# Attention with head pairs in the halves of the array: scores in two banks, values stationary in column halves, gates and y feature-major

## The chip, the core and the metric

The kernel runs on one core of a Trainium2 chip. A core has five engines with their own queues of instructions: PE (TensorE, matrix products; the loads of its stationary operand are listed as PEld), DVE (VectorE), ACT (ScalarE), POOL (GpSimd) and SP (here only a queue of DMAs). Each engine works through its queue in order and waits on semaphores. The metric is the device time of one execution in microseconds; less is better.

## What is computed

The input is 256 tokens of 1024 features. Two layers of a first block, then two of a second, all in float32. The parts that the change touches, from the reference:

```python
# first block, per layer (8 heads of 64 in a and b, 4 of 128 in the memory branch)
qa, ka = partial_rope(a_q), partial_rope(a_k)
ya = moba_attention(qa, ka, va) * silu(a_g)          # causal softmax attention at this length
rel = relu(einsum('bqhd,bsd->bqhs', qi, ki))
idx_score = einsum('bqhs,bqh->bqs', rel, wi)         # its 64 largest keys per query are kept
yb = dsa_attention(qb, kb, vb, qi, ki, wi) * silu(b_g)
ym = memory_attention(m_q, km, vm) * silu(m_g)       # 256 memory rows, no mask
up = einsum('bsnw,nwd->bsnd', stack([ya, yb, ym]), w_branch)
merged = sum(sigmoid(mix) * up)
x = x + merged @ w_out
# second block, per layer: three mixers side by side, then a feed-forward network
o = gt[..., 0:1] * o_cmp + gt[..., 1:2] * o_slc + gt[..., 2:3] * o_win   # NSA mixer, 8 heads of 64
mix = concatenate([o_gla, o_rwkv, o_nsa]) @ w_out
```

## The kernel before, in words

Tokens stand in two tiles of 128 (`tt`). Activations are held feature-major (features on the partitions, 256 tokens in the columns) as operands of the next product, in two parts, high and low, that together carry all bits of the float32 values (class `Feat`, made by `put`, L1395: four transposes on PE, then `split`, one copy on ACT and one subtraction on DVE).

**Weights.** All weights come as one stream in the order in which they are used. `unit` (L250) issues a DMA of 128x1024 on SP's queue into `raw`, ACT makes `whi` (L267) and DVE `wlo` (L244, the helper `tt_`, where most of DVE's elementwise work is recorded). `mm3` (L277) makes three matmuls of each product (L280, L281, L282). A projection is either token-major (`proj_tok`: tokens stationary, 512 weight columns moving) or feature-major (`proj_feat`: weights stationary, the 256 tokens moving).

**Attention of 8 heads of 64** (`causal_attn`, L477). Queries and keys are feature-major, so heads of even number stand on partitions 0 to 63 and those of odd number on 64 to 127. A group is four heads of one parity for the first token tile (128 keys) and two heads for the second (256 keys): two groups for `tt` = 0, four for `tt` = 1. Per group: scores (L490, half of the array's rows), the mask as one more product added into the same bank (L493 causal, L496 index mask), then `softmax_pv` (L456): maximum (L461), its negative (L463), one exponential per head on ACT with the sum of the row beside it (L467), transposes of the unscaled exponentials (L350, the helper `transposed`), a copy to SBUF (L471), and the product with values (L474: transposed exponentials stationary, 64 columns of values moving, result token-major). Branch a and b end in `gate_out` (L500): reciprocal of the sums (L503), y = o / sum, times the gate, and `put`. The memory branch does the same with four heads of 128 (L590). The NSA mixer of block 2 uses `causal_attn` twice per token tile (selected and window), each with its own bank, divisor and sum in SBUF, and a compressed branch (`nsa_compressed`, L1200; products with values L1231).

**The index mask** (`index_mask`, L511): scores (L524) as half-array products, relu on ACT (L527), a weighted sum of eight heads in `iacc` (L532 for the first, L247 for the rest) on DVE, and eight rounds of the eight largest (L544, L545) in `iwork` on DVE.

**PSUM.** Four pools of banks: `pp` 2, `pr` 2, `pa` 3, `pg` 1. `self.ps` takes from `pa`: the result `o` of an attention, the scores of a group and the transposes share its three banks.

**Order.** The program is written as in the source, and a scheduler orders each engine's instructions by priority: a part stands where it is written, moved ahead by `AHEAD[name]` instructions of the section that it is written in (atta -57, attb -195, imask -501, nsa 126, rwkv 38, and so on). So attention, index mask and projections interleave. The table is the same before and after.

Of the kernel before, what the change touches and what calls it, by code (L numbers as in the profile page):

```python
# [113 lines left out]
def consts():  # L114
    c = {}
# [34 lines left out]
class Kern:  # L150
# [48 lines left out]
    def sec(self, name):  # L199
        """a part of the program that is scheduled as if it stood AHEAD[name] instructions earlier"""  # L200
# [5 lines left out]
    def block(self, bufs):  # L206
        """buffers of one block, by tag; streams that run beside each other share no tag"""
# [31 lines left out]
    def accs(self):  # L239
        """[tt][cg] for 1024 columns"""  # L240
# [36 lines left out]
    def mm3(self, out, a, b, start, stop):  # L277
        """out += (ah + al).T @ (bh + bl); the parts carry all bits of the float32 operands"""
# [29 lines left out]
    def proj_feat(self, tag, xT, done, pool, kch=8):  # L308
        """feature-major: out[c] = (x @ W).T for chunks of 128 columns; done(pair, psum[128, 2, 256])"""
# [36 lines left out]
    def transposed(self, ps, srcs):  # L346
        """up to four [128, 128] -> psum [128, n, 128]"""
# [5 lines left out]
    def transp(self, src, dst, tt):  # L353
        """src [128 tok, 512] -> dst[:, 0:4, tt] (float32)"""
# [3 lines left out]
    def bcast(self, ap_row, eng=None):  # L358
        """a row of 1024 for all partitions, in two halves"""
# [6 lines left out]
    def rms(self, xs, g, xT, ps=None, out=None):  # L366
        """x (+= ps) -> split transposes of rmsnorm(x) * g in xT, or the rows in out"""
# [1126 lines left out]
```

## Time and profile before

| | us |
|---|---|
| median of three runs | 1593.73 (1588.67 to 1603.2) |
| span of the profiled execution | 1594.3 |
| PE busy | 1554.3 (97%) |
| PE's stationary loads | 1357.4 (85%) |
| DVE busy | 1018.5 (64%) |
| ACT busy | 719.7 (45%) |

PE's busy share is near the whole; its weight loads run beside its matmuls. A float32 matmul that isn't split by hand is recorded as two. Lengths of matmuls in the trace overlap (their ends are modelled), so what one costs is read from where the next one starts. Next to the engine times the profile has the granted clock of PE, 1 being full speed.

### The profile page before, as it was taken

What the parts mean: (1) busy time and instruction counts of PE and PEld (TensorE: products, weight loads), DVE (VectorE), ACT (ScalarE), POOL (GpSimd) and SP (SyncE); (2) the same over time, 40 slices, a digit from 0 to 9 for tenths busy, and PEclk for the clock granted to TensorE, in tenths of its full rate; (3) what the DMA queues carried; (4) which work ended last, traced back from release to release, by engine and by line L of the source; (5) the groups of instructions that cost most, each with busy time, mean ns of one, the idle gap of its engine ahead of it and who ended that gap; (6) DMA issues with size and microseconds to landing.
All of it is one profiled execution on the core that took longest, in us unless ns stands there. A gap on an engine that the chain in (4) does not pass through costs nothing.

```text
span 1594.3 us, 24848 instructions
## 1 busy us (share of the span) xinstructions
PE 1554.3 (97%) x9868; PEld 1357.4 (85%) x9868; DVE 1018.5 (64%) x1645; ACT 719.7 (45%) x1266; POOL 43.9 (3%) x82
## 2 busy tenths in 40 slices
PE   7999999999999999999999999999999999999998
PEld 6877889989878899979878779999798687789987
DVE  5668556575586565665768685556758786665565
ACT  5544444445544444445644234445346442334451
POOL 0000000000000000010000000000000000100000
PEclk9999999999999999999979999999999998799999
DMA  8642435446534335565212245547353121254661
GB/s 275 229 163 90 153 106 169 162 171 210 182 108 143 107 121 184 191 194 176 91 42 81 71 127 196 188 167 240 129 170 103 54 67 67 67 197 165 200 220 38
DMA packets 72836, 231.78 MB, mean 145 GB/s; under 512 B 8592, under 2 KB 11280, under 8 KB 72720
## 3 DMA queue, kind: packets, MB, share of 16 engines
q1 hardware_dynamic: 67248, 219.74, 41.4%
q10 hardware_dynamic: 5472, 10.46, 2.1%
q8 instruction: 77, 1.26, 0.3%
q14 instruction: 39, 0.32, 0.1%
HBM read 229.12 MB, written 1.05 MB: 144 GB/s over the span
## 4 chain that ended last, share of the span: by engine, by line
PE 86%; DVE 5%; DMA 4%; ACT 3%; issue 1%; POOL 0%; ACTq 0%; SPq 0%; DVEq 0%; POOLq 0%
PE ps L282 21%; PE ps L281 21%; PE ps L280 21%; PE ps L350 5%; PE ps L474 3%; PE ps L490 3%; DMA raw<-in_stream_dram 3%; PE ps L1045 2%; DVE wlo L244 1%; ACT whi L267 1%; PE ps L858 1%; PE ps L880 1%; PE ps L1138 1%; PE ps L826 1%; PE ps L524 1%
## 5 line engine op out<-in xcount | busy, mean ns | idle before, releaser
L244 DVE TENSOR_TENSOR wlo<-raw,whi 128x1024 fp32r<-128x1024 f32 (+2 forms) x396 | 466.7, 1186 | 304.7 <-ACT whi L267 301.9
L267 ACT CAST whi<-raw 128x1024 fp32r<-128x1024 f32 (+2 forms) x396 | 401.5, 1021 | 406.7 <-PE ps L282 164.8
L280 PE MATMUL ps<-xTh,whi 128*128 128x256 f32 (+1 forms) x784 | 224.8, 287 | 4.1 <-ACT whi L267 4.1
L282 PE MATMUL ps<-xTh,wlo 128*128 128x256 f32 (+1 forms) x784 | 224.0, 286 | 0.7 <-DVE wlo L244 0.5
L281 PE MATMUL ps<-xTl,whi 128*128 128x256 f32 (+1 forms) x784 | 223.9, 286 | 0.0
L280 PEld LDWEIGHTS ps<-xTh,whi 128*128 128x128 f32 (+1 forms) x784 | 150.6, 192 | 7.5 <-ACT whi L267 4.5
L282 PEld LDWEIGHTS ps<-xTh,wlo 128*128 128x128 f32 (+1 forms) x784 | 150.4, 192 | 2.8 <-DVE wlo L244 1.2
L281 PEld LDWEIGHTS ps<-xTl,whi 128*128 128x128 f32 (+1 forms) x784 | 150.7, 192 | 0.3
L282 PE MATMUL ps<-whi,hTl 128*128 128x512 f32 (+2 forms) x352 | 135.4, 385 | 0.0
L280 PE MATMUL ps<-whi,hTh 128*128 128x512 f32 (+2 forms) x352 | 135.1, 385 | 0.0
L281 PE MATMUL ps<-wlo,hTh 128*128 128x512 f32 (+2 forms) x352 | 134.6, 382 | 0.0
L282 PE MATMUL ps<-hTh,wlo 128*128 128x256 f32 x448 | 128.9, 288 | 0.0
L280 PE MATMUL ps<-hTh,whi 128*128 128x256 f32 x448 | 128.8, 287 | 0.0
L281 PE MATMUL ps<-hTl,whi 128*128 128x256 f32 x448 | 128.2, 286 | 0.0
L467 ACT ACTIVATE pexp<-ps,nb 128x256 f32<-128x256 f32 (+1 forms) x144 | 59.8, 425 | 66.6 <-DVE nb L463 59.6
L280 PEld LDWEIGHTS ps<-hTh,whi 128*128 128x128 f32 x448 | 85.9, 192 | 0.7
L281 PEld LDWEIGHTS ps<-hTl,whi 128*128 128x128 f32 x448 | 85.8, 191 | 0.7
L282 PEld LDWEIGHTS ps<-hTh,wlo 128*128 128x128 f32 x448 | 85.8, 192 | 0.3
L280 PEld LDWEIGHTS ps<-whi,hTh 128*128 128x128 f32 x352 | 66.1, 188 | 11.9 <-issue 2.0
L281 PEld LDWEIGHTS ps<-wlo,hTh 128*128 128x128 f32 x352 | 66.4, 189 | 11.3 <-issue 0.7
L282 PEld LDWEIGHTS ps<-whi,hTl 128*128 128x128 f32 x352 | 66.3, 188 | 10.9
L280 PE MATMUL ps<-whi,xTh 128*128 128x512 f32 (+1 forms) x176 | 69.8, 397 | 1.4 <-ACT xTh L340 1.3
(447 smaller groups left out, 3076.3 us busy)
## 6 DMA issues: line engine op xcount, KB each, us to landing
raw<-in_stream_dram SPq DMA_DIRECT2D x368, 512.0 KB, 4.0
raw<-in_stream_dram SPq DMA_DIRECT2D x56, 256.0 KB, 3.1
row<-in_ln_w_dram ACTq DMA_DIRECT2D x8, 256.0 KB, 4.7
row<-in_ln_b_dram ACTq DMA_DIRECT2D x8, 256.0 KB, 5.6
raw<-in_stream_dram SPq DMA_DIRECT2D x4, 480.0 KB, 4.6
raw<-in_stream_dram SPq DMA_DIRECT2D x4, 420.0 KB, 3.6
raw<-in_stream_dram SPq DMA_DIRECT2D x4, 396.0 KB, 5.0
P<-in_p_dram ACTq DMA_DIRECT2D x2, 668.5 KB, 5.4
```

What stands on the lines that cost most here:

```text
L244: self.nc.vector.tensor_tensor(out=out, in0=a, in1=b, op=op)
L267: nc.scalar.copy(hi[:, :b - a], raw)
L280: mm(out, a[0], b[0], start=start, stop=False)
L281: mm(out, a[0], b[1], start=False, stop=False)
L282: mm(out, a[1], b[0], start=False, stop=stop)
L350: self.nc.tensor.transpose(pt[:, j], s, self.ident)
L467: nc.scalar.activation(p3[:, i], sv[:, i], AF.Exp, bias=nb[:, i:i + 1], scale=scale, accum_out=den[:, h:h + 1])
L474: nc.tensor.matmul(o[:, ocol(h)], ps[:, i * nk + k, :], vt(k, h), start=first and i == 0 and k == 0, stop=last and i == nh - 1 and k == nk ...
L490: nc.tensor.matmul(s3[:, i], qT[pr, h // 2], kT(pr, h, 128 * nk), start=i == 0, stop=False)
L524: nc.tensor.matmul(s3[:, i], iqT[pr, h // 2, 128 * tt:128 * tt + 128], ikT[pr, :n], start=i == 0, stop=i == hs - 1)
L826: mm(ps[:, c], st[pr, c, 128 * tt:128 * tt + 128], ar4[tt][pr, :, c, :], start=c == 0, stop=c == 1)
L1045: mm(ps[:, tt, c], E[pr, c, sl], E[pr, c, sl], start=tt + c == 0, stop=tt + c == 2)
```

## The change

- `causal_attn` takes heads in pairs: scores of both parities go into two banks, in turn. `softmax_pv` becomes `probs`: the reciprocal of the row sums (L476), in block 2 times the mixer's gate, is multiplied into the exponentials (L480, one instruction a head) before their transposes. The product with values (L510) has 64 columns of values stationary in one half of the array's columns and 128 tokens moving; even heads give partitions 0 to 63 of the result and odd ones 64 to 127. The result is feature-major.
- `gate_proj`: the three gates of a block-1 layer are projected feature-major. `gate_out` multiplies the feature-major result by them and splits it, with no transposes of y.
- `nsa_direct`: selected and window attention add into one bank; ACT copies the sum. `nsa_compressed` scales its probabilities, makes its products in column halves (32 of them), adds and splits; no `put` of yn, and no section "ofn".
- `index_mask` issues the scores of both parities in turn, into two banks.
- Comments and docstrings are taken out.

Between the orders of before and after: 48 transposes of yb and 16 of yn are gone; 288 weight matmuls of 512 columns became 576 of 256; 384 matmul records of values have 128 moving columns instead of 64; on DVE there are 144 more scalings and 56 reciprocals in place of 20. The DMAs are the same.

```diff
-    def softmax_pv(self, sv, heads, nk, scale, vt, o, ocol, den, first, last):
+    def probs(self, sv, coef, scale):
 ...
-        for i, h in enumerate(heads):
-            nc.scalar.activation(p3[:, i], sv[:, i], AF.Exp, bias=nb[:, i:i + 1], scale=scale,
-                                 accum_out=den[:, h:h + 1])
-        pt = self.transposed(self.ps, [p[:, 128 * j:128 * j + 128] for j in range(nh * nk)])
+        for i in range(nh):
+            nc.scalar.activation(p3[:, i], sv[:, i], AF.Exp, bias=nb[:, i:i + 1], scale=scale, accum_out=den[:, i:i + 1])
+        rd = self.sm.tile([128, 4], F32, name="rd")
+        nc.vector.reciprocal(rd[:, :nh], den[:, :nh])
+        if coef is not None:
+            self.tt_(rd[:, :nh], rd[:, :nh], coef, ALU.mult)
+        for i in range(nh):
+            nc.vector.tensor_scalar(p3[:, i], p3[:, i], rd[:, i:i + 1], None, op0=ALU.mult)
+        pt = self.transposed(self.ps, [p[:, 128 * j:128 * j + 128] for j in range(nh * n // 128)])
         ps = self.u("ptsb", 4, 128)
         nc.vector.tensor_copy(ps, pt)
-                nc.tensor.matmul(o[:, ocol(h)], ps[:, i * nk + k, :], vt(k, h),
-                                 start=first and i == 0 and k == 0, stop=last and i == nh - 1 and k == nk - 1)
 ...
+            sv = [self.ps(hs, 128 * nk) for _ in par]
+            for i in range(hs):
+                for a, pr in enumerate(par):
+                    h = g + 2 * i + a
+                    nc.tensor.matmul(sv[a][:, i], qT[pr, h // 2], kT(pr, h, 128 * nk), start=i == 0, stop=False)
 ...
+            pT = [self.probs(sv[a], coef[:, g + a:g + 2 * hs:2] if coef is not None else None, 0.125) for a in range(2)]
+            for i in range(hs):
+                for k in range(nk):
+                    for a, pr in enumerate(par):
+                        nc.tensor.matmul(o[pr, g // 2 + i], v(k, g + 2 * i + a), pT[a][:, i * nk + k],
 ...
-        self.tt_(y.rearrange("p (h d) -> p h d", h=nh), o.rearrange("p (h d) -> p h d", h=nh),
-                 rd[:, :nh, None].to_broadcast([128, nh, d]), ALU.mult)
-        self.tt_(y, y, g2, ALU.mult)
-        ysT.put(y, 0, tt, 0.5)
+        for p in range(2):
+            self.tt_(y[:, 2 * p:2 * p + 2], o[:, 2 * p:2 * p + 2], g2[p][:, :, sl], ALU.mult)
+        self.split(y, ysT.h[0][:, :, sl], ysT.l[0][:, :, sl], 0.5)
 ...
-            g2 = self.tok_proj(f"{n}g{l}", hT, "g", self.silu2)
+            g2 = self.gate_proj(f"{n}g{l}", hT)
 ...
+            self.nc.scalar.copy(out[tt], o)
 ...
-            for g in range(2):
-                mm(oc[:, g], pT[:, g], vc[g], start=g == 0, stop=g == 1)
+            for j in range(4):
+                for g in range(2):
+                    mm(oc[64 * g:64 * g + 64, j], vc[g][:, j], pT[:, g], start=j == 0, stop=j == 3)
```

How the order changes, at three places of the first layer (a row is a line, an operation, output<-inputs, shape, and how many follow each other; a float32 matmul is one row here and two records in the trace).

PE, where branch a begins, before: index scores (L524) stand among the weight matmuls (L280 to L282) and the first scores (L490).

```order
L524 MATMUL ps<-ikT,iqT 128x256
L280 MATMUL ps<-whi,hTh 128x512
L524 MATMUL ps<-ikT,iqT 128x256
L281 MATMUL ps<-wlo,hTh 128x512
L282 MATMUL ps<-whi,hTl 128x512
L524 MATMUL ps<-ikT,iqT 128x256 x4
L280 MATMUL ps<-whi,hTh 128x512
L281 MATMUL ps<-wlo,hTh 128x512
L524 MATMUL ps<-ikT,iqT 128x256
L490 MATMUL ps<-kT,qT 128x128 x4
```

The same place after: index scores (now L533) and the scores (now L499) with their causal mask (L502).

```order
L533 MATMUL ps<-ikT,iqT 128x128 x8
L533 MATMUL ps<-ikT,iqT 128x256 x6
L499 MATMUL ps<-kT,qT 128x128 x4
L502 LDWEIGHTS negb
L502 MATMUL ps<-causb,negb 128x512
L533 MATMUL ps<-ikT,iqT 128x256 x2
L280 MATMUL ps<-whi,hTh 128x512
L281 MATMUL ps<-wlo,hTh 128x512
L499 MATMUL ps<-kT,qT 128x128 x4
```

The index scores moved together, 14 of a layer's 16 in one block, behind the end of the gates' projection; the first two groups' scores follow each with its mask.

PE, a little later, after: the products with values of the first pair (L510, `ptsb` being the transposed probabilities) and the scores of the second pair (L499); what each waits for is in brackets.

```order
L350 MATMUL ps<-c_ident,pexp 128x128 [waits DVE_49,Activation_49]
L510 MATMUL ps<-ptsb,v 64x128 [waits PE_49]
L350 MATMUL ps<-c_ident,pexp 128x128 [waits DVE_49] x3
L499 MATMUL ps<-kT,qT 128x256 [waits Activation_49]
L499 MATMUL ps<-kT,qT 128x256
L502 LDWEIGHTS negb
L502 MATMUL ps<-causb,negb 128x2x128
L281 MATMUL ps<-wlo,hTh 128x512
L510 MATMUL ps<-ptsb,v 64x128 [waits DVE_49]
L510 MATMUL ps<-ptsb,v 64x128 x6
L499 MATMUL ps<-kT,qT 128x256 [waits PE_49]
L499 MATMUL ps<-kT,qT 128x256
```

One product stands by itself and seven follow later, where before each group had its four together. The second bank's scores stand behind the first bank's and behind the products.

DVE in that stretch, before: between the rounds of the first index selection (L544, L545) stand pieces of the weights (wlo).

```order
L544 MAX m_663<-iacc 128x8
L545 MATCH_REPLACE iwork<-m_663,iacc 128x128
L244 TENSOR_TENSOR wlo<-raw,whi 128x1024
L544 MAX m_663<-iwork 128x8
L545 MATCH_REPLACE iwork<-m_663,iwork 128x128
L544 MAX m_663<-iwork 128x8
L545 MATCH_REPLACE iwork<-m_663,iwork 128x128
L544 MAX m_663<-iwork 128x8
L545 MATCH_REPLACE iwork<-m_663,iwork 128x128
L244 TENSOR_TENSOR wlo<-raw,whi 128x1024
```

After: the rounds of both selections (now L555, L556) stand among the softmax's pieces.

```order
L480 TENSOR_SCALAR pexp<-pexp,rd 128x128 x4
L469 TENSOR_SCALAR nb<-mx 128x4
L555 MAX m_663<-iwork 128x8
L247 SCALAR_TENSOR_TENSOR iacc<-irel,wi,iacc 128x256
L483 COPY ptsb<-ps 128x512
L556 MATCH_REPLACE iwork<-m_663,iwork 128x128
L555 MAX m_715<-iacc 128x8
L555 MAX m_663<-iwork 128x8
L556 MATCH_REPLACE iwork<-m_715,iacc 128x256
L476 RECIPROCAL rd<-den 128x4
L556 MATCH_REPLACE iwork<-m_663,iwork 128x128
L480 TENSOR_SCALAR pexp<-pexp,rd 128x128 x4
```

No wlo stands from the first index sum to the end of the second selection; before, one stood every few rows.

## Rows read from the trace of the kernel before

**Rows 1.** The page's part 1: busy time, share of span, instructions of each engine.
```profile
PE 1554.3 (97%) x9868; PEld 1357.4 (85%) x9868; DVE 1018.5 (64%) x1645; ACT 719.7 (45%) x1266; POOL 43.9 (3%) x82
```

**Rows 2.** The page's part 4: the chain that ended last, by engine.
```profile
PE 86%; DVE 5%; DMA 4%; ACT 3%; issue 1%; POOL 0%; ACTq 0%; SPq 0%; DVEq 0%; POOLq 0%
```

**Rows 3.** Stretches: length, busy PE, PEld, DVE, ACT, POOL, granted clock, DMA share, GB/s.
```profile
110.00:160.00 50.00, 50.00 (x269) 38.07 (x268) 40.92 (x112) 23.99 (x56) 0.58 (x2) 1.00 0.30 102
809.30:833.20 23.90, 23.23 (x97) 19.57 (x96) 13.92 (x27) 9.39 (x20) 0.00 (x0) 0.50 0.07 23
1345.20:1375.90 30.70, 30.59 (x107) 24.03 (x107) 13.00 (x25) 2.75 (x6) 1.64 (x1) 0.50 0.05 21
```

**Rows 4.** Timeline of PE at 159 us: start, length, line, shape, count.
```profile
159.19 0.40 PE L282 MATMUL ps<-whi,hTl 128*128 128x512 f32 x1
159.42 0.60 PE L350 MATMUL ps<-c_ident,yb 128*128 128x128 f32 x4
159.78 0.48 PE L280 MATMUL ps<-whi,hTh 128*128 128x512 f32 x1
```

**Rows 5.** Timeline of PE at 180 us: narrow weight matmuls and single scores.
```profile
179.88 0.28 PE L282 MATMUL ps<-hTh,wlo 128*128 128x256 f32 x1
180.00 0.28 PE L280 MATMUL ps<-hTh,whi 128*128 128x256 f32 x1
...
180.63 0.39 PE L281 MATMUL ps<-hTl,whi 128*128 128x256 f32 x1
...
181.36 0.38 PE L282 MATMUL ps<-hTh,wlo 128*128 128x256 f32 x1
```

**Rows 6.** Timeline of PE from 102 us: index scores of a block-1 layer.
```profile
102.12 0.49 PE L524 MATMUL ps<-ikT,iqT 64*128 64x128 f32 x2
...
102.97 0.49 PE L524 MATMUL ps<-ikT,iqT 64*128 64x128 f32 x2
...
117.79 1.14 PE L524 MATMUL ps<-ikT,iqT 64*128 64x256 f32 x8
```

**Rows 7.** Timeline of PE at 188 us: one group's products, another's scores.
```profile
187.80 1.10 PE L474 MATMUL ps<-v,ptsb 128*128 128x64 f32 x8
188.83 1.16 PE L490 MATMUL ps<-kT,qT 64*128 64x128 f32 x8
```

**Rows 8.** Timeline of PE at 906 us: alternating column halves, and what follows.
```profile
905.58 0.66 PE L949 MATMUL ps<-r_M,r_WU 128*64 128x128 f32 x8
906.17 1.10 PE L955 MATMUL ps<-r_WU,r_M 128*128 128x64 f32 x8
```

**Rows 9.** Timeline of DVE at 130 us: weights, reciprocal, copy of transposes.
```profile
129.98 1.21 DVE L244 TENSOR_TENSOR wlo<-raw,whi 128x1024 fp32r<-128x1024 f32 x1
...
131.50 0.19 DVE L503 RECIPROCAL rd<-den 128x8 f32<-128x8 f32 x1
131.63 0.69 DVE L471 COPY ptsb<-ps 128x512 f32<-128x512 f32 x1
```

**Rows 10.** Timeline of ACT at 130 us: exponentials of one softmax.
```profile
129.71 0.37 ACT L467 ACTIVATE pexp<-ps,nb 128x128 f32<-128x128 f32 x1
...
130.06 0.36 ACT L467 ACTIVATE pexp<-ps,nb 128x128 f32<-128x128 f32 x1
```

**Rows 11.** Line L532: durations in ns (minimum, median, maximum), forms.
```profile
L532 DVE TENSOR_SCALAR iacc<-irel,wi x4: 286/312/335, 105.8 to 455.0; 128x128 f32<-128x128 f32 x2, 128x256 f32<-128x256 f32 x2
```

**Rows 12.** Line L467: who waited for it (us, times).
```profile
  PEld ps L350: 8.2, 25
```

**Rows 13.** Busy DVE (last row third) from 100 us on iacc, iwork, mx, ptsb.
```profile
100.00:160.00 60.00, 8.59 (x24) 0.58 (x2) 1.00 0.32 109
...
100.00:160.00 60.00, 12.31 (x48) 1.00 0.32 109
...
100.00:160.00 60.00, 5.11 (x12) 1.00 0.32 109
...
100.00:160.00 60.00, 6.43 (x48) 5.89 (x48) 4.12 (x6) 1.00 0.32 109
```

More of the change, by code (lines that the diff above doesn't have):

```diff
@@ L448, in tok_proj, with gate_proj @@
         return dst
+    def gate_proj(self, tag, hT):
+        g2 = [self.u("g", 2, 256) for _ in range(2)]
+        self.proj_feat(tag, hT, lambda p, ps: self.silu2(g2[p], ps), self.next_pool())
+        return g2
     def silu2(self, dst, ps):
-        t = self.u("tg")
+        t = self.u("tg", 2, 256)
         self.nc.scalar.activation(t, ps, AF.Tanh, scale=0.5)
         self.stt(dst, t, 1.0, ps, ALU.add, ALU.mult)
-    def softmax_pv(self, sv, heads, nk, scale, vt, o, ocol, den, first, last):
+    def probs(self, sv, coef, scale):
         nc = self.nc
-        nh = len(heads)
+        nh, n = sv.shape[1], sv.shape[2]
         mx = self.sm.tile([128, 4], F32, name="mx")
@@ L465, in softmax_pv, with causal_attn @@
         p3 = p.rearrange("p (h k) -> p h k", h=nh)
-        for i, h in enumerate(heads):
-            nc.scalar.activation(p3[:, i], sv[:, i], AF.Exp, bias=nb[:, i:i + 1], scale=scale,
-                                 accum_out=den[:, h:h + 1])
-        pt = self.transposed(self.ps, [p[:, 128 * j:128 * j + 128] for j in range(nh * nk)])
+        den = self.sm.tile([128, 4], F32, name="den")
+        for i in range(nh):
[7 more added lines that the diff above has]
+        pt = self.transposed(self.ps, [p[:, 128 * j:128 * j + 128] for j in range(nh * n // 128)])
         ps = self.u("ptsb", 4, 128)
         nc.vector.tensor_copy(ps, pt)
-        for i, h in enumerate(heads):
-            for k in range(nk):
-                nc.tensor.matmul(o[:, ocol(h)], ps[:, i * nk + k, :], vt(k, h),
-                                 start=first and i == 0 and k == 0, stop=last and i == nh - 1 and k == nk - 1)
-    def causal_attn(self, qT, kT, v, tt, o, den, mask=None):
+        return ps
+    def causal_attn(self, qT, kT, v, tt, o, first, last, mask=None, coef=None):
         nc = self.nc
@@ L481, in causal_attn @@
         hs = 4 // nk
[L482 removed]
+        par = (slice(0, 64), slice(64, 128))
         for g in range(0, 8, 2 * hs):
[L484 to L498 removed]
@@ new lines, in causal_attn @@
+            for i in range(hs):
+                for a, pr in enumerate(par):
+                    h = g + 2 * i + a
+                    nc.tensor.matmul(sv[a][:, i], qT[pr, h // 2], kT(pr, h, 128 * nk), start=i == 0, stop=False)
+            for s3 in sv:
+                if mask is None:
+                    nc.tensor.matmul(s3[:, :, 128 * tt:128 * tt + 128], self.negb,
+                                     self.causb[:, None, :].to_broadcast([128, hs, 128]), start=False, stop=True)
+                else:
+                    nc.tensor.matmul(s3, self.negb, mask[:, None, :].to_broadcast([128, hs, 128 * nk]), start=False, stop=True)
@@ L1204, in nsa_compressed @@
         for tt in range(2):
-            acc = out[tt]
             den = self.sm.tile([128, 8], F32, name="n_cden")
@@ L1221, in nsa_compressed @@
             self.tt_(cf, cf, gate[:, 0], ALU.mult)
+            self.tt_(s, s, cf[:, :, None].to_broadcast([128, 8, 15]), ALU.mult)
             pc = self.u("n_pc", 2, 4, 32)
@@ L1228, in nsa_compressed @@
             nc.scalar.copy(pT, pt)
-            oc = self.ps(2, 4, 64)
-            for g in range(2):
-                mm(oc[:, g], pT[:, g], vc[g], start=g == 0, stop=g == 1)
-            t = self.u("n_t", 4, 2, 64)
-            c3 = cf.rearrange("p (j g) -> p g j", g=2)
-            for g in range(2):
-                self.tt_(t[:, :, g], oc[:, g], c3[:, g, :, None].to_broadcast([128, 4, 64]), ALU.mult)
-            self.tt_(acc, acc, t.rearrange("p j g d -> p (j g d)"), ALU.add)
+            oc = self.ps(4, 128)
+            for j in range(4):
+                for g in range(2):
+                    mm(oc[64 * g:64 * g + 64, j], vc[g][:, j], pT[:, g], start=j == 0, stop=j == 3)
+            self.tt_(out[tt], out[tt], oc, ALU.add)
+            sl = slice(128 * tt, 128 * tt + 128)
+            self.split(out[tt], yT.h[0][:, :, sl], yT.l[0][:, :, sl])
     def block2_layer(self, l, xT):
@@ L1251, in block2_layer @@
         yr, yg = self.c3("yr"), self.c3("yg")
-        yn = [self.u("yn") for tt in range(2)]
+        yn = [self.u("yn", 4, 128) for tt in range(2)]
         qT, kT, KX, vt, gc = self.nsa_inputs(l, xT)
@@ L1265, in block2_layer @@
         with self.sec("cpd"):
-            self.nsa_compressed(qT, gc, kc, vc, yn)
-        with self.sec("ofn"):
             yT = Feat(self, 4, "xT")
-            for tt in range(2):
-                yT.put(yn[tt], 0, tt)
+            self.nsa_compressed(qT, gc, kc, vc, yn, yT)
         with self.sec("h1"):
```

76 lines of the change are left out of this document (25 added, 51 removed).

## The prediction

> **What bounds the kernel now.** I read the engine totals first [rows 1]: PE is busy 1554.3 of 1594.3 us, DVE 64% and ACT 45% of the span. The chain that ended last [rows 2] says the same: 86% of it is PE, 5% DVE. So the time is PE's list of instructions, plus 40 us in which PE waits. Then I looked at the one stretch of a block-1 layer where DVE is nearly as full: from 110 to 160 us [rows 3] PE is busy all 50 us, and DVE 40.92. There the index mask, the attention of branch a and the splitting of the weights (wlo) share DVE. In block 2 two stretches of 24 and 31 us run at a granted clock of 0.50 [rows 3], the lower level of 1.2 GHz, while PE is busy nearly all the time; what lengthens them is paid double. The profiled span of 1594.3 us stands 0.6 us above the median of the runs, so differences worked out on the trace go against the median, 1593.7, as they are.
>
> **Part 1: what PE no longer does.** The transposes of y go: 48 of yb and 16 of yn. A group of four between weight matmuls takes PE from 159.42 to 159.78, 0.09 us each [rows 4]; sixteen such groups are about 6 us, and 7 with what they cost on entry. I take -7.
>
> The gates change shape: 288 weight matmuls of 512 columns become 576 of 256. Pitches are 0.23 us [rows 4] and 0.12 us [rows 5], so 576 x 0.119 - 288 x 0.231 is +2.
>
> The products with values: a group of 8 records (four matmuls of 64 columns, two records each because they are plain float32) takes 0.91 to 1.1 us; the one at 187.80 holds PE until 188.83 [rows 7]. There are 48 such groups, some 46 us. After the change a pair of groups is 16 records of 128 columns into alternating column halves, issued as one single (2 records) and one run of 14, as the excerpt of the order on the first pair's products shows. The nearest row is the stretch of L949, which has just this form: 8 records from 905.58 to 906.17 [rows 8], that is four pitches of 0.11 and 0.15 for entering and leaving. Seven pitches and 0.15 are 0.93 us; the single has to be entered and left by itself, about 0.46. 24 x (0.46 + 0.93) = 33, so -12. If only one half runs at a time, 16 x 0.11 + 0.3 a pair gives 50, so +4; if the single costs nothing extra, -15.
>
> Here a rule of the Trainium skill speaks against the change. The row shows 0.15 us around the L949 group. The page TensorEngine Tiling (Array Packing), section Key Properties, says that changing the tiling mode drains TensorE, and the groups that did not change mode before now do so twice a pair. It gives no price; with another 0.28 for each of the 48 entries, what the lone half-row group at 188.83 pays beyond its columns (1.16 - 8 x 0.11, [rows 7]), the part's gain would be about 0 instead of -12.
>
> The scores: the code alternates the two row halves, but o, two score banks and the transposes share the three banks of one PSUM pool. In the same excerpt the scores into the second bank stand behind those into the first, their mask and the products, with a wait of their own. So a group still costs what it costs now, 1.1 us (1.16 with its modelled end) at 188.83 [rows 7], except where both banks happen to be free. The index scores are such a place. Before, most were singles between weight matmuls: a single and a weight matmul take 0.85 us [rows 6], so the single costs 0.62, and a layer's sixteen about 8.5. After, 14 of them stand in one block and alternate halves: by the run at 117.79, 8 records of 256 columns in 1.14 [rows 6], the block is about 2.6. That is -6 a layer. Against it, in branch b the first pair's scores become eight singles among weight matmuls instead of four and a group: from 180.63 to 181.36 less 0.12 makes 0.61 each [rows 5], four times 0.61 less 1.1, and the same once more in part for block 2: about +2.5 a layer. Sum -7, bounds -3 and -12.
>
> The compressed branch's 8 wide matmuls become 32 small ones: +1. In all PE has 23 us less to do (-7 + 2 - 12 - 7 + 1), bounds -6 and -34.
>
> **Part 2: what DVE gets.** Every probability is now scaled before its transpose: a reciprocal, and 64 multiplications of 128 columns and 80 of 256. The same form, an elementwise multiply with a scalar per row, took 0.286 and 0.335 us in L532 [rows 11]. Against this the divisions at the end of a branch and the n_t sums go, and the gate products read half as much. Net about +20 us on DVE, at a share of 64%. Over most of the kernel PE's queue of weight matmuls hides that. Two places don't.
>
> First, branch a of each block-1 layer. In the order before, wlo pieces stand between the pieces of the index mask. After, there is none between the one ahead of the index block and the one behind the second imask. DVE has there the index sums and the selection, 8.59 + 12.31 us less about 1.6 counted in both [rows 13], the maxima of six softmax calls 5.11, five of the six copies of 4.12 [rows 13], and newly some 5 us of scaling, 1 of reciprocals, 0.8 and 0.7 for y and its split, 1 of rope: about 36 us by durations. An instruction's successor starts some 0.08 us before its end (131.50 with 0.19, next at 131.63 [rows 9]), times 90 that is 7: 29 us, and with the wlo that ends it 30 to 31 after the first index score. PE has in the same stretch 48 weight matmuls (11.1), the index block (2.6 and some 1.5 of waits for the relu), six groups of scores with masks (7), transposes (2.6) and values (2.8): about 26 to 27 before it needs that wlo. PE waits 4.5 us, twice: +9, bounds 0 (if the weights' buffers carry it over) and +16 (if the selection's steps wait for each other).
>
> Second, the softmax chain. Before, the first transpose could follow the first exponential; the pitch of these is 0.35 us [rows 10]. Now it follows all of a group's exponentials, a reciprocal of 0.19 [rows 9] and a scaling: about 1.5 us later with four heads of 128, 1.1 with two of 256, in 56 calls. The order gives part of it back, since in branch b 27 to 31 narrow weight matmuls stand where 20 stood. The trace of before shows 8.2 us of waits for pexp in 25 places [rows 12]; I take half as much again, +4, bounds 0 and +20.
>
> In block 2 the pairs come later: two or three are still to come when the last weight matmuls are gone, before it was two. They share DVE with rwkv there. I take +2, bounds -5 and +15, the half of the longer slow-clock stretch.
>
> The edit's other pieces (ACT splits y from SBUF instead of PSUM, four copies of yn) lie on ACT at 45% [rows 1] and cost nothing as long as no transpose waits for them; uncovered they would be 16 x 0.69 by the copy of that size at 131.63 [rows 9], 11 us. DMA is the same list.
>
> **Sum.** -23 + 9 + 4 + 2 = -8, so about 1585 us.
>
> **Rivals.** (1) The cover holds: the wlo pieces made ahead and the reordered weight matmuls hide both DVE places. For it: DVE has a third of its time free and the order moved fillers to where the transposes are. Against it: no wlo in 29 us of DVE work. Then -23 and 0 to +3 remain: 1571 to 1574. (2) Slower: the longer softmax chain is exposed everywhere. In each of 56 calls a reciprocal and scalings now stand behind a wlo of 1.2 us [rows 9] where one comes between exponentials and transposes. Uncovered by half, 0.65 us a call, it is +36 instead of +4: 1594 - 23 + 9 + 36 + 2 = 1618. It decides when a call's exposure passes 0.5 us (28 + 11 - 23 = +16, one per cent). For it: the two halves of a pair share three banks, so a pair's chain can't be started ahead; against it: only 8.2 us are waited there now. (3) The change doesn't do what it says: each of the 48 entries into column halves costs another 0.28 us and eats the gain, so -11 of PE work against +15: about 1598. Against it stands the L949 row [rows 8], where 8 records took 0.59 us against 1.03 in the whole array [rows 7].
>
> **How the numbers follow.** Forecast 0.42, between 1575 and 1597 by its own terms; rival 1 0.25; rival 2 0.16; rival 3 0.17. About one per cent, 16 us, is what a measurement of this kernel tells from no change. Faster by more than that (under 1578) are nearly all of rival 1 and a fifth of the forecast: 0.32. Slower (over 1610) is rival 2: 0.15. The rest, 0.53, is within it. The range of 1565 to 1613 leaves out the best end of rival 1 and most of rival 2, about 2 in 10.
>
> **What would show it.** Right: no L350 on yb or yn; the values' runs of 14 records in about 0.9 us; index scores in a block of about 3 us soon after 100 us; DVE over 90% busy there and PE waiting 4 to 5 us for a wlo just behind it, twice; waits of transposes for pexp of 10 to 15 us in all. Wrong: values at 1.5 us or more a pair (rival 3), waits for pexp of 30 us and more (rival 2), or none for that wlo (rival 1); and a granted clock of 0.50 in block 2 over another length than 24 and 31 us would move the time by half the difference.

## The result, and the profile of the changed kernel

The changed kernel takes 1613.45 us in the median of 11 runs (1604.5 to 1616.6), the kernel before 1596.9 beside it on the same chip. The ratio is 1.0093, with an interval of 1.0068 to 1.0118: 15 us slower, where 9 us faster was forecast. Medians, ratios and parts of time are here and below those of fast runs alone; a run over 1.5% above the fastest of its kernel counts as slow. The profiled execution has a span of 1614.7 us against 1594.3.

The engine totals (the page's part 1) and the chain that ended last (part 4; here it is followed back through 63% of the span only, so its shares are small):

```profile
PE 1560.7 (97%) x10140; PEld 1361.4 (84%) x10140; DVE 1034.8 (64%) x1825; ACT 722.5 (45%) x1270; POOL 46.0 (3%) x82
```

```profile
PE 53%; DVE 4%; DMA 3%; ACT 2%; issue 1%; POOL 0%; ACTq 0%; DVEq 0%; POOLq 0%; SPq 0%
```

Against [rows 1] DVE has 16 us more (20 were forecast) and keeps its share. PE's busy time should have fallen by 23 and rose by 6. Busy time hides how fast the work ran; the stretches tell it. Columns as in [rows 3]: length, busy PE, PEld, DVE, ACT, POOL, granted clock, DMA share, GB/s. The last lines are those of the stretches that lie at the lower level in the changed kernel:

```profile
110.00:160.00 50.00, 47.49 (x253) 36.17 (x252) 40.48 (x122) 22.80 (x47) 0.29 (x1) 1.00 0.31 106
170.00:180.70 10.70, 10.70 (x75) 9.36 (x73) 5.59 (x6) 4.24 (x5) 0.00 (x0) 1.00 0.51 177
180.70:187.50 6.80, 6.80 (x23) 5.15 (x23) 1.56 (x4) 0.97 (x6) 0.00 (x0) 0.50 0.20 66
795.00:802.00 7.00, 7.00 (x31) 5.26 (x30) 3.97 (x6) 3.89 (x8) 0.00 (x0) 0.51 0.26 84
812.00:826.00 14.00, 13.62 (x50) 9.00 (x49) 8.76 (x22) 2.95 (x9) 2.23 (x4) 0.51 0.00 0
918.00:935.00 17.00, 13.83 (x48) 11.62 (x49) 9.06 (x18) 2.09 (x6) 3.32 (x2) 0.50 0.04 15
1266.00:1287.00 21.00, 21.00 (x82) 15.04 (x80) 10.57 (x30) 6.23 (x18) 2.66 (x4) 0.51 0.00 1
1314.00:1324.00 10.00, 10.00 (x44) 9.30 (x42) 5.00 (x16) 3.19 (x12) 0.40 (x1) 0.50 0.00 1
1365.00:1396.00 31.00, 28.59 (x104) 22.61 (x104) 13.17 (x25) 2.64 (x6) 2.08 (x2) 0.50 0.00 1
```

With a second one like that at 180.70, at 519, and some short ones, 125 us lie at 0.50; before it was 77. Block 1 had none before: in the kernel before, the stretches 180.70 to 187.50 and 519 to 526 have 1.00 (46 and 51 matmuls on PE, here 23 and 29 in about as long).

What that costs can be read from the runs alone, since each lists its span and mean granted clock. Call (1 - clock) x span the time lost. Over 179 runs of the ten kernels with ten or more of them, a run's span stands above its own kernel's mean by 0.78 us for each us that its lost time stands above that kernel's mean (correlation 0.97). So I divide a kernel's difference to before (medians: span 1593.2, lost 33.5, 82 runs) into 0.8 times the difference in lost time, "the clock", and "the rest", what remains at equal clock. That the factor holds from kernel to kernel as it does from run to run is assumed. For the changed kernel: span 1611.7, lost 58.0, so +18.5 us, of which 0.8 x 24.5 = 20 are the clock, and the rest is -1. The forecast had +2 for the clock and -10 for everything else. Both parts are off, the first by 18 us, the second by 9.

### The profile page after: what moved, and what is told of

Read it like the earlier page. It is cut to its first block, busy times and chain, and to the rows that moved or that the text cites. A ratio compares the mean times of both kernels' runs of the same rounds, so it can differ in the third digit from the quotient of the medians.

```text
span 1614.7 us, 25573 instructions
## 1 busy us (share of the span) xinstructions
PE 1560.7 (97%) x10140; PEld 1361.4 (84%) x10140; DVE 1034.8 (64%) x1825; ACT 722.5 (45%) x1270; POOL 46.0 (3%) x82
## 4 chain that ended last, share of the span: by engine, by line
PE 53%; DVE 4%; DMA 3%; ACT 2%; issue 1%; POOL 0%; ACTq 0%; DVEq 0%; POOLq 0%; SPq 0%
PE ps L280 12%; PE ps L282 12%; PE ps L281 12%; PE ps L350 3%; DMA raw<-in_stream_dram 3%; PE ps L1057 2%; PE ps L499 2%; DVE wlo L244 1%; PE ps L510 1%; PE ps L892 1%; PE ps L870 1%; ACT whi L267 1%; PE ps L838 1%; PE ps L1150 1%; PE ps L881 1%
## 5 line engine op out<-in xcount | busy, mean ns | idle before, releaser
L244 DVE TENSOR_TENSOR wlo<-raw,whi 128x1024 fp32r<-128x1024 f32 (+2 forms) x396 | 467.5, 1190 | 319.1 <-ACT whi L267 317.8
L280 PE MATMUL ps<-xTh,whi 128*128 128x256 f32 (+1 forms) x784 | 224.3, 286 | 4.8 <-ACT whi L267 4.6
L282 PE MATMUL ps<-xTh,wlo 128*128 128x256 f32 (+1 forms) x784 | 223.7, 286 | 0.8 <-DVE wlo L244 0.8
L281 PE MATMUL ps<-hTl,whi 128*128 128x256 f32 x640 | 184.9, 289 | 0.0
L282 PE MATMUL ps<-hTh,wlo 128*128 128x256 f32 x640 | 184.8, 289 | 0.0
L280 PE MATMUL ps<-hTh,whi 128*128 128x256 f32 x640 | 184.5, 288 | 0.0
L280 PEld LDWEIGHTS ps<-xTh,whi 128*128 128x128 f32 (+1 forms) x784 | 150.4, 192 | 9.2 <-ACT whi L267 5.0
L282 PEld LDWEIGHTS ps<-xTh,wlo 128*128 128x128 f32 (+1 forms) x784 | 150.4, 192 | 3.2 <-DVE wlo L244 1.5
L282 PEld LDWEIGHTS ps<-hTh,wlo 128*128 128x128 f32 x640 | 124.0, 194 | 1.8 <-issue 0.8
L281 PEld LDWEIGHTS ps<-hTl,whi 128*128 128x128 f32 x640 | 124.1, 194 | 1.4 <-issue 0.4
L280 PEld LDWEIGHTS ps<-hTh,whi 128*128 128x128 f32 x640 | 124.1, 194 | 1.2 <-issue 0.6
L281 PE MATMUL ps<-wlo,hTh 128*128 128x512 f32 (+2 forms) x256 | 95.1, 372 | 2.1 <-DVE wlo L244 2.1
L282 PE MATMUL ps<-whi,hTl 128*128 128x512 f32 (+2 forms) x256 | 95.6, 373 | 0.0
L280 PE MATMUL ps<-whi,hTh 128*128 128x512 f32 (+2 forms) x256 | 94.6, 372 | 0.0
L280 PE MATMUL ps<-whi,xTh 128*128 128x512 f32 (+1 forms) x176 | 69.7, 397 | 3.8 <-ACT xTh L340 2.6
L281 PE MATMUL ps<-wlo,xTh 128*128 128x512 f32 (+1 forms) x176 | 69.1, 392 | 0.9 <-DVE wlo L244 0.9
L282 PE MATMUL ps<-whi,xTl 128*128 128x512 f32 (+1 forms) x176 | 69.3, 394 | 0.1
L467 DVE TENSOR_REDUCE mx<-ps 128x2 f32<-128x512 f32 (+1 forms) x56 | 38.2, 688 | 38.7 <-PE ps L502 19.9
```

What stands on the lines that cost most here:

```text
L244: self.nc.vector.tensor_tensor(out=out, in0=a, in1=b, op=op)
L280: mm(out, a[0], b[0], start=start, stop=False)
L281: mm(out, a[0], b[1], start=False, stop=False)
L282: mm(out, a[1], b[0], start=False, stop=stop)
L467: nc.vector.tensor_reduce(out=mx[:, :nh], in_=sv, axis=AX.X, op=ALU.max)
```

## The experiments

The suspects in the order in which they came: the place of the added scores in branch b, the place of NSA in block 2, the two score banks, the scaling of the probabilities. The table gives for each kernel the ratio to before with its interval, and the two parts, in us, as above. (From run to run of one kernel the rest scatters by 1 to 2 us; a factor of 0.7 or 0.9 in place of 0.8 would shift it by up to 2.5 us. On the four chips of the experiments the kernel before has the same at equal clock within 0.4 us.)

| kernel | median us | ratio | interval | clock | rest |
|---|---|---|---|---|---|
| the changed kernel | 1613.5 | 1.0093 | 1.0068-1.0118 | +20 | -1 |
| e1_attb: branch b later | 1598.9 | 1.0033 | 1.0003-1.0064 | +15 | -11 |
| e2_nsa: NSA earlier | 1606.4 | 1.0106 | 1.0030-1.0182 | +14 | -2 |
| e3_before_pair: before, two banks | 1599.4 | 1.0056 | 1.0012-1.0101 | -3 | +7 |
| e4_noscale: no scaling | 1595.8 | 1.0014 | 0.9969-1.0058 | +6 | -6 |
| e5_block1: block 1 only | 1599.7 | 1.0058 | 1.0020-1.0096 | +9 | -4 |
| e6_block2: block 2 only | 1608.3 | 1.0071 | 1.0037-1.0105 | +13 | 0 |
| e7_block1_attb: e5 and e1 | 1583.2 | 0.9931 | 0.9891-0.9971 | +3 | -15 |
| e8_block2_noscale: e6, no scaling | 1601.2 | 1.0049 | 1.0010-1.0089 | +1 | +5 |
| e9_block2_act: e6, scaling on ACT | 1619.0 | 1.0142 | 1.0092-1.0193 | +20 | +4 |
| e10_nsa170: e1, NSA earlier | 1593.1 | 0.9972 | 0.9945-0.9999 | +12 | -14 |
| e11_nsa200: e1, NSA earlier still | 1586.7 | 0.9980 | 0.9939-1.0021 | +4 | -12 |
| e12_before_table: before, e11's table | 1598.1 | 1.0007 | 0.9967-1.0047 | 0 | +3 |

A trace, on the other hand, is of one execution, and executions of one kernel differ in clock (the kernel before from 0.967 to 0.990). So a stretch's clock in one trace against that in another says little by itself; the table decides.

**Branch b's scores.** One entry of the table that sets the order is changed.

```diff
-AHEAD = dict(... attb=-195, ...)
+AHEAD = dict(... attb=-135, ...)
```

> The changed kernel with one number of the order table altered (attb from -195 to -135): in branch b of both block-1 layers the first pair's eight scores stand together instead of alternating one by one with narrow weight matmuls; block 2 is ordered as in the changed kernel. Theory C (stretches in which PE is poorly filled make the granted clock fall, and the falls are the loss): the two stretches of 6.8 us at 0.50 near 181 and 519 us are gone, 3.4 us each, and with them seven singles at some 0.5 us a layer; about 14 us faster than the changed kernel, 1600 us. Theory D (the longer softmax chain and DVE are the loss): within 3 us of the changed kernel, 1611 to 1616 us.

In the changed kernel the first pair's eight scores of branch b stand one by one among narrow weight matmuls. The timeline of PE (start, length, line, operation, shape, records):

```profile
177.09 0.48 PE L499 MATMUL ps<-kT,qT 64*128 64x128 f32 x2
177.50 0.39 PE L281 MATMUL ps<-hTl,whi 128*128 128x256 f32 x1
177.82 0.48 PE L499 MATMUL ps<-kT,qT 64*128 64x128 f32 x2
...
180.01 0.48 PE L499 MATMUL ps<-kT,qT 64*128 64x128 f32 x2
180.42 0.39 PE L282 MATMUL ps<-hTh,wlo 128*128 128x256 f32 x1
180.74 0.79 PE L499 MATMUL ps<-kT,qT 64*128 64x128 f32 x2
181.46 0.58 PE L280 MATMUL ps<-hTh,whi 128*128 128x256 f32 x1
181.97 0.79 PE L499 MATMUL ps<-kT,qT 64*128 64x128 f32 x2
```

Each single and its weight matmul take 0.73 us, and from the sixth on 1.23: there the granted clock falls to 0.50, and stays there for 6.8 us. The same happens in the second layer at 519. The trace shows no wait of PE in the 10.7 us before the fall (ends of matmuls are modelled). With the entry changed, the eight stand together, and the same part of both layers keeps its clock (stretches of e1_attb):

```profile
170.00:190.00 20.00, 19.40 (x157) 16.99 (x156) 15.15 (x34) 10.78 (x31) 0.00 (x0) 1.00 0.35 118
505.00:530.00 25.00, 24.33 (x185) 20.71 (x185) 17.01 (x42) 12.85 (x37) 0.00 (x0) 1.00 0.33 107
```

So the entry is worth 15 us of span, 4 by the clock and 10 at equal clock in the table. The two traces show where: the last matmul on the y of block 1 (`ps<-ysh,wlo`) starts at 667.3 us in the changed kernel and at 653.3 in e1_attb, so 14.0 of the 15 us arise before block 2, half in each layer. Of the 7 us of a layer 3.4 are half speed; eight singles at 0.61 [rows 5] in place of one row of 16 records that takes 1.09 us (171.32 to 172.41 in e1_attb) are 3.8, an estimate.

**NSA earlier in block 2.**

```diff
-AHEAD = dict(... nsa=126, ...)
+AHEAD = dict(... nsa=190, ...)
```

> The changed kernel with the NSA attention of block 2 moved ahead (nsa from 126 to 190), so that all its pairs lie among weight matmuls and none among rwkv's last steps. Theory C: the time at 0.50 in block 2 (85 us without the ends, 68 before the change) shrinks to 60 or less, 10 to 17 us faster than the changed kernel, about 1600 us. Theory D: the chain of a pair is as long, its waits now fall among weight matmuls; at most 5 us faster, 1608 us or more.

Only four runs stand behind it, so the interval is wide. The medians say that a third of the clock's cost goes (20 to 14) and the rest stays; whether the kernel is faster than the changed one these runs don't tell. Theory C's 10 to 17 us did not come, and the trace, that of the slowest of the four, has no less time at 0.50 in block 2 (a clock of 0.91 from 770 to 1400 us, 0.92 in the changed kernel).

**Two score banks alone, in the kernel before.**

```diff
-        for gi, heads in enumerate(groups):
-            s3 = self.ps(hs, 128 * nk)
 ...
+            sv = [self.ps(hs, 128 * nk) for _ in par]
+            for i in range(hs):
+                for a, pr in enumerate(par):
+                    h = g + 2 * i + a
+                    nc.tensor.matmul(sv[a][:, i], qT[pr, h // 2], kT(pr, h, 128 * nk), start=i == 0, stop=False)
 ...
```

> The kernel before with one part of the change alone: scores of both parities issued in turn into two banks, everything behind them as before (no scaling, transposes of y, token-major gates). Its order has 64 single half-array scores among other matmuls, before 32. Theory C: the clock falls in branch b and in block 2 as after the change; 10 to 15 us slower than before, 1607 to 1612 us. Theory D: the softmax chain is the old one, so no more than the singles themselves, 32 at 0.2 to 0.5 us less what alternating halves save: 1594 to 1604 us.

It has 64 single half-array scores (those of the index mask among them) where before has 32, and it is 7 us slower at equal clock, but its clock is no lower than before's in the median. 32 singles at 0.61 in place of eight groups at 1.1 would be some 11 us, an estimate from [rows 5] and [rows 7]; so the singles are enough to explain the loss, and two banks by themselves gain nothing. It has the same eight singles in branch b as the changed kernel, and its trace (that of its lowest clock, 0.961) falls at the same place of the first layer, for 3.4 us:

```profile
182.56 0.69 PE L488 MATMUL ps<-kT,qT 64*128 64x128 f32 x2
183.18 0.58 PE L282 MATMUL ps<-hTh,wlo 128*128 128x256 f32 x1
```

```profile
182.80:186.20 3.40, 3.40 (x14) 2.69 (x14) 1.56 (x4) 1.07 (x2) 0.00 (x0) 0.51 0.00 0
```

In its second layer, with the same eight from 514 to 520 us, it does not fall. Counted over all fourteen traces: where six to eight of these scores stand one by one (the changed kernel, e2, e3, e4, e5), the clock falls at them in nine of ten layers; where four do or none (the nine others), in none of eighteen. In block 2 the singles of e3_before_pair (22, before has 2) leave the median clock as it was, so singles alone are no rule.

**Without the scaling.** This kernel leaves out the division by the sums of the softmax.

```diff
-for i in range(nh):
-    nc.vector.tensor_scalar(p3[:, i], p3[:, i], rd[:, i:i + 1], None, op0=ALU.mult)
```

> The changed kernel without the 144 scalings of the probabilities (the division by the row sums is left out, so the output is not the reference's); the transposes again follow the exponentials. Theory D: the loss goes, 15 us or more faster than the changed kernel, under 1599 us. Theory C: the waits that the scalings cause go, some 3 us a block-1 layer and as much in block 2, but the order still has 42 single scores; 4 to 10 us faster, 1603 to 1609 us.

It gains 17.7 us on the changed kernel by the medians of the span, 13 of them the clock. That is the time that theory D had. But the order changes with it too (42 singles), so it doesn't tell whether the work on DVE, the longer chain or the order did it.

**One block at a time.** The other block keeps the code of before (its softmax, gates and, in e6, the transposes of yb; in e5 those of yn).

> The change in block 1 alone (branches a, b, memory, index scores, gates); block 2's mixers as before, ordered as in the kernel before. Theory C (the loss is the granted clock, most of it in block 2): block 1 has at equal clock 2 to 3 us less a layer and pays 3.4 us a layer for the stretch at 0.50 in branch b, so 1592 to 1600 us, the same as before. Theory S (the loss is the single half-array scores and the waits of block 1): 8 us or more slower than before, 1603 us or more.

> The change in block 2 alone (NSA mixer); block 1 as before, ordered as in the kernel before. Theory C: most of the loss, 10 to 18 us slower than before, 1605 to 1613 us, with more time at 0.50 than the 65 us of before between 790 and 1400 us. Theory S: within 5 us of before, 1590 to 1600 us.

Block 1 is worth +5 us, block 2 +13, and the sum of 18 is that of the whole change. Block 1's share is a clock cost of 9 with a rest of -4, and its profile has the two stretches at 180 and 518. Block 2's share is all clock. In its trace, that of its lowest clock (0.964), the two attention stretches stand at 0.86 and 0.79, where the kernel before has 0.90 (790 to 940) and 0.88 (1240 to 1385). Stretches of e6_block2, of the same columns:

```profile
790.00:945.00 155.00, 148.33 (x904) 119.11 (x905) 107.95 (x222) 54.68 (x118) 12.43 (x25) 0.86 0.21 67
1260.00:1400.00 140.00, 135.49 (x800) 110.87 (x797) 88.45 (x187) 42.81 (x96) 8.63 (x13) 0.79 0.13 43
```

**Block 1 with its scores together.** e5_block1 with the edit of e1_attb.

> As the run with the change in block 1 alone, with attb at -135 as well, so that branch b's first eight scores stand together. Both theories: 10 to 15 us faster than that run, for the singles and the clock behind them; by theory C 1580 to 1587 us, faster than before by some 10 us; by theory S 1590 to 1597 us.

This beats both kernels: 0.9931 of the time of before, about 11 us. The clock is that of before within 3 us, and the rest is -15. Block 1's mechanism is there, and its loss was the place of eight scores in each layer. The traces agree: the last matmul on the y of block 1 starts at 653.3 to 654.2 us in e1, e7, e10 and e11, at 664.4 to 665.9 in the five with block 1 as before (before, e6, e8, e9, e12), and at 665.9 to 669.5 in e5, the changed kernel and e2, with the singles. The stretches of e7_block1_attb that answer to 180.70 and to the first of block 2:

```profile
170.00:190.00 20.00, 19.41 (x157) 16.99 (x156) 14.99 (x33) 10.44 (x31) 0.00 (x0) 1.00 0.37 128
790.00:925.00 135.00, 127.15 (x838) 104.61 (x838) 104.15 (x201) 53.52 (x109) 12.01 (x25) 0.97 0.24 76
```

Its block 2 is the code of before, and yet the second stretch has 0.97 where before's has 0.90. Since the medians of the two kernels' clocks differ by less than 0.003, that is within what one kernel shows from run to run, and no effect of block 1.

**What lowers block 2's clock: the scaling?** e6_block2 without it (this kernel leaves out the same division in block 2), and with it on ACT.

```diff
-nc.vector.tensor_scalar(p3[:, i], p3[:, i], rd[:, i:i + 1], None, op0=ALU.mult)
+nc.scalar.activation(p3[:, i], p3[:, i], AF.Copy, scale=rd[:, i:i + 1])
```

> As the run with the change in block 2 alone, without the scalings of the probabilities (left out, so the output is not the reference's). If the longer softmax chain is what empties PE and lowers the clock in block 2: 8 us or more faster than that run, 1600 us or less. If the half-array matmuls and single scores lower the clock by themselves, whatever the chain: within 4 us of that run, 1603 us or more.

> As the run with the change in block 2 alone, with the scalings of the probabilities done on ACT instead of DVE. The softmax chain of a pair is not shorter (a pass of 0.35 to 0.46 us on ACT for one of 0.25 to 0.33 on DVE), but DVE has some 10 us less to do in block 2. Theory L (the chain's length empties PE and lowers the clock): no faster than that run, 1604 to 1612 us. Theory V (DVE's load does it, since rwkv's steps wait for DVE too): 6 us or more faster, 1602 us or less.

Without the scaling the clock's cost goes from 13 to 1, but the rest goes from 0 to +5, so that only 7 us of span are gained, between the two expectations. With the scaling on ACT the kernel is slower, 1619 us in four runs, its clock cost 20. Two suspects lose by this. DVE's load: DVE has that work no longer (ACT has it instead). And the wait of the transposes for the probabilities: that is 11.4 us in e6_block2, 6.4 in e8, and 7.4 in e9, so e9 waits nearly as little as e8 and has as low a clock as the whole change (0.964 in the median). Who waited for pexp, in e6_block2 and then in e9_block2_act:

```profile
  PEld ps L350: 7.4, 19
...
  PE ps L350: 4.0, 3
```

```profile
  PEld ps L350: 6.9, 23
...
  PE ps L350: 0.5, 2
```

Each of these is one execution (clocks 0.964, 0.981 and 0.970), and the order in which block 2 runs is moved by each of the edits. So the order is the suspect that is left; these runs don't show it by themselves. The stretches of e8_block2_noscale:

```profile
790.00:945.00 155.00, 145.34 (x910) 118.70 (x909) 107.66 (x209) 56.50 (x115) 15.49 (x28) 0.91 0.24 78
1260.00:1400.00 140.00, 134.59 (x833) 110.87 (x833) 103.86 (x195) 51.52 (x98) 10.70 (x13) 0.91 0.21 69
```

**The order alone, in the whole change.** e1_attb's edit, and NSA at 170 or 200 instead of 126; and the last table with the code of before.

```diff
-AHEAD = dict(... attb=-195, ..., nsa=126, ...)
+AHEAD = dict(... attb=-135, ..., nsa=200, ...)
```

> The whole change with two numbers of the order table altered: attb -135 and nsa 170 (NSA attention some 44 instructions earlier, its pairs among weight matmuls until the last). If the clock of block 2 is lost where pairs lie beside rwkv's last steps: 8 us or more under the run with attb alone, 1591 us or less. If it is lost wherever a pair's chain is exposed: within 4 us of that run, 1595 to 1603 us.

> As the run before, with nsa at 200: the pairs another 30 instructions earlier, all but the last among weight matmuls. By the first view 1591 us or less, by the second 1595 to 1603 us.

> The kernel before with the two numbers of the order table that the last run has (attb -135, nsa 200) and nothing of the change. If the gain of that run over before comes from the table: some 8 us faster than before, 1588 us or less. If it comes from the change, once its pairs stand where the clock holds: within 4 us of before, 1591 to 1600 us, since in this kernel the four singles in branch b stay and its pairs were among weight matmuls already but for the last two.

Nothing is left out here and no instruction is added: from e1_attb over e10 to e11 only NSA moves, the rest stays at -11 to -14, and the clock goes from +15 over +12 to +4. The medians of the span follow: 1597.2, 1591.3, 1584.9. (By means instead of medians the clock is +14, +12 and +6. e10 came out between its two expectations, e11 within the first.) The stretches of e11_nsa200, whose trace is of its highest clock, 0.979:

```profile
770.00:935.00 165.00, 156.52 (x962) 129.84 (x961) 118.80 (x236) 65.66 (x131) 13.51 (x27) 0.89 0.23 73
1245.00:1370.00 125.00, 116.64 (x789) 96.57 (x788) 91.68 (x182) 48.03 (x98) 9.58 (x12) 0.93 0.16 56
```

Waits don't order these kernels: the transposes wait 13.7 us for the probabilities in the trace of e1, 6.2 in e10 and 7.8 in e11. Nor does PE's standing still: by the lines shown e11 stands still for 16.8 of 290 us and e6_block2 for 11.2 of 295, and e11 has the higher clock (a faster PE may also wait more). e11's ratio is 0.9980 with an interval that holds 1, so it isn't shown faster than before, though it is faster than the changed kernel. The same table does nothing for the code of before (1.0007), so what e10 and e11 regain is the change's own.

## Why the prediction was wrong, step by step

**PE's work.** The transposes of yb and yn are gone: no line L350 on either is left. The products with values take what was worked out. In branch a of the first layer:

```profile
115.26 0.43 PE L510 MATMUL ps<-ptsb,v 128*64 128x128 f32 x2
115.63 0.55 PE L350 MATMUL ps<-c_ident,pexp 128*128 128x128 f32 x3
...
117.61 1.09 PE L510 MATMUL ps<-ptsb,v 128*64 128x128 f32 x14
118.63 0.91 PE L499 MATMUL ps<-kT,qT 64*128 64x256 f32 x3
```

0.37 from start to start for the single and 1.02 for the run are 1.39 a pair; 0.46 + 0.93 was the forecast, from [rows 8]. Rival 3, with another 0.56 a pair, falls by it. That the sum agrees is in part luck: two records more take 0.11 us ((1.02 - 0.37) / 6), so 0.26 remain for entering and leaving, where the forecast had 0.15 at the run and more at the single. The Trainium skill has the rule that changing the tiling mode drains TensorE (page TensorEngine Tiling (Array Packing), section Key Properties). These 0.26 us are the most that it can cost in this row. The forecast's bounds for PE's work were added up wrongly, too: its parts give -31 and -3, not -34 and -6. The index scores were mis-sized:

```profile
101.39 3.74 PE L533 MATMUL ps<-ikT,iqT 64*128 64x128 f32 x28
105.28 1.16 PE L499 MATMUL ps<-kT,qT 64*128 64x128 f32 x8
106.37 0.39 PE L502 MATMUL ps<-causb,negb 128*128 128x512 bf16 x1
106.69 0.70 PE L533 MATMUL ps<-ikT,iqT 64*128 64x256 f32 x4
```

The block takes 3.89 us from start to start and two more scores 0.63, 4.5 in all against 2.6 in the forecast: -4 a layer, not -6.

**The wait in branch a.** DVE is as full as forecast: from 101.40 to 135.00 us it is busy 31.65 of 33.6. The imasks and the wlo that comes behind stand where they were expected (first DVE, then PE, with the idle time before an instruction and its releaser in brackets):

```profile
133.49 0.41 DVE L244 TENSOR_TENSOR imask<-iwork,iacc 128x256 bf16<-128x256 f32 x1
133.82 1.22 DVE L244 TENSOR_TENSOR wlo<-raw,whi 128x1024 fp32r<-128x1024 f32 x1
```

```profile
131.87 0.63 PE L350 MATMUL ps<-c_ident,pexp 128*128 128x128 f32 x4 [0.90 <-DVE pexp L480]
...
133.63 0.43 PE L510 MATMUL ps<-ptsb,v 128*64 128x128 f32 x2 [0.34 <-DVE ptsb L483]
135.10 0.50 PE L281 MATMUL ps<-wlo,hTh 128*128 128x512 f32 x1 [1.03 <-DVE wlo L244]
```

PE waits 2.3 us there, and as much ahead of the same weight matmul of the second layer (472.47 us), half of the 4.5, because its own work in that stretch is 31 us and not 26 to 27. (The forecast's own addends make 27.6, which would have left a wait of 3.) Over all, this layer is 2.3 us ahead of before at 163 us, by the same weight matmul in both traces: up to there the forecast's mechanism is right and its sign too.

**The softmax chain.** Waits of the transposes for the probabilities are 12.5 us (who waited for whom, us in total, times, longest):

```profile
PE ps L350 <- DVE pexp L480: 7.6, 11, 1.9
...
PEld ps L350 <- DVE pexp L480: 4.9, 9, 2.0
```

Before, 8.2 were on PEld [rows 12], and 2.1 more on PE, which the forecast left out. So +2, not +4; rival 2, which needed 0.5 us in each of 56 calls, falls, though its side of the result came.

**Branch b.** The forecast saw the eight singles and priced them at +2.5 us a layer, by [rows 5], at the upper level of the clock. Between 163 and 188 us the kernel goes from 2.3 us ahead to 4.0 behind: 6.3 us. 3.4 of them are the 6.8 us at half speed. Of the remaining 2.9, 0.6 come before the singles, from the gates' narrower matmuls; 1.1 are the four scores that the kernel before makes only at 188.83 [rows 7]; and some 1.3 are the forecast's price for the first pair, four times 0.61 less 1.1. So this term failed by the clock, which it took as given: 3.4 us in each layer that it put at nothing. e1_attb shows the two layers' worth, 14.0 us, by putting the eight scores together.

**Block 2's clock: the step that failed.** "I take +2, bounds -5 and +15, the half of the longer slow-clock stretch" took the two stretches of [rows 3] as they were and let one grow or shrink. Of these the one of 24 us became two, of 7 and 14 us, from 795 on, and the one of 31 us stayed. But one of 7 us at 919 grew to 17, and from 1266 and 1314 on there are new ones of 21 and 10 us, where before had 3. Clock cost in block 2 is 13 us, in block 1 it is 9 by e5 (where the forecast had no term at all), 20 for both. The prediction named this as a sign of its being wrong, and the half of the difference that it gave fits: between 770 and 1400 us 102 us lie at 0.50, before 68, and half of the difference is 17 us in this pair of executions. Two waits of PE for the scaled probabilities stand ahead of such places:

```profile
793.33 0.44 PE L350 MATMUL ps<-c_ident,pexp 128*128 128x128 f32 x2 [1.54 <-DVE pexp L480]
...
1254.41 0.63 PE L350 MATMUL ps<-c_ident,pexp 128*128 128x128 f32 x4 [1.92 <-DVE pexp L480]
```

The clock falls at 795.1, close behind the first of these (before, it fell only at 809); behind the second it falls only at 1266, after 10 us of work in small pieces. The Trainium skill (page TensorE: Matmul & The Clock Gate, section HAM oscillation — how this bites in real kernels) lays falls of the clock to waits of PE between groups of matmuls. At 793 there is such a wait, of 1.54 us, ahead of the fall; that it is the cause isn't shown. At 180.70 there is none: PE was busy for all of the 10.70 us before it. And e9_block2_act and e10_nsa170, with short waits and a low clock, speak against the waits as the cause in block 2 as a whole. What exactly in the order brings the clock down there is not settled: shown is that moving NSA alone (e1_attb, e10, e11) takes the cost from 15 to 4 us with the same instructions.

**The gain in block 2.** At equal clock e6_block2 is at 0 where the forecast's terms for it (16 transposes, half of the values, less its bits of chain) come to some -6. In the two traces PE stands still for 20.6 us in the two NSA parts after the change (677 to 960 and 1195 to 1415 us) and for 14.8 before (677 to 950 and 1190 to 1400), which is about what is missing. e3_before_pair and e8_block2_noscale, at +7 and +5, have singles in block 2 (22 each, before has 2), which may be their price; what e8's +5 is made of isn't shown.

**The sum.** At equal clock the change brings -1 as made and -11 with branch b's scores together, where the forecast without its clock term was -10. That -11 lies near -10 is luck: the forecast had +5 in it for the singles, which e1_attb doesn't have, so without them its terms make about -15. The index scores and block 2 gave less than forecast (4 and 6 us), the wait in branch a and the chain cost less (4 and 2). For block 1 alone the terms make some -4 (-10 without block 2's -6), which is what e5_block1 has; there the sum holds at equal clock (e7, with the clock kept and the singles gone, has 1581 us of span), and the changed kernel doesn't keep its clock.

## What to carry to other kernels

Where a kernel is bound by PE and its trace has stretches at 0.50, the granted clock is a term of the sum of its own, with bounds that take in the stretches whose order the change alters, not only those already slow. Divide each run's difference into lost time (1 - clock) x span and a rest before looking for a cause: the two answer to different edits. And an order that is set by a table kept from the old code has to be set again for the new before the change is judged; here two numbers of it were worth 27 us by the medians of the span, 18 by the two ratios to before.

## What the runs showed of the hardware

The mean granted clock of one kernel differs from run to run (0.962 to 0.971 in the changed kernel, 0.967 to 0.990 in the kernel before), and the span follows it by 0.78 us for each us lost (correlation 0.97 over 179 runs), closely enough that two kernels can be compared at equal clock. At 0.50 a single score and its weight matmul went from 0.73 to 1.23 us. The clock can fall while the trace shows PE busy without a gap, as at 180.70; with six to eight single scores among narrow weight matmuls it fell so in nine of ten layers, with the scores together in none. One and the same code can get different clocks, as block 2 of before in the traces of before and of e7_block1_attb (0.90 and 0.97 in its first stretch). Entering and leaving alternating column halves took 0.26 us among other matmuls, 0.15 in the one place where the kernel before had it.
